# Seven products instead of eight in the second MLP matrix of a decoder trunk, with weight sums formed by adding DMAs

## Chip, cores and metric

One core of one Trainium2 chip runs the whole program. The metric is device time in microseconds (us); lower is better. Engines: PE = TensorE, DVE = VectorE, ACT = ScalarE, POOL = GpSimd, SP = SyncE, which only issues DMAs here.

## The reference

Two layers over 1,024 positions of width 1,024, in float32. Layer 0 mixes by sliding-window attention beside a gated delta rule, layer 1 by a gated recurrence (RG-LRU). Every layer ends with the same MLP of width 4,096, which the change is about:

```python
def sqrelu_mlp(x, w1, w2):
    h = jax.nn.relu(x @ w1)
    return (h * h) @ w2

def reference(x, ...):
    for layer in range(DEPTH):
        ...
        x = layer_norm(DN_ALPHA * x + mix, ln1_g[layer], ln1_b[layer])
        x = layer_norm(DN_ALPHA * x + sqrelu_mlp(x, mlp_w1[layer], mlp_w2[layer]), ln2_g[layer], ln2_b[layer])
    return x
```

## The kernel before

The sequence is cut into two halves of 512 positions (c = 0 and 1). Each half is a Python generator (`stream`): hybrid mixer, layer norm, MLP, recurrent mixer, layer norm, MLP, layer norm. A driver at the end of the function steps the generators and, between them, small ones (`mixers`: attention, delta rule, layer norms). It takes the half in the lower phase first whenever that one is not blocked, so one half's mixer lies among the other half's MLP products. A class `Clock` keeps rough times of all engines and fixes the order of PE's instructions; the other engines' instructions are put in order by the framework's scheduler.

Every matrix product of float32 values is done as three products of float32r values: each operand is split into a high part (a cast) and a low part (the operand minus its high part), and `mm3` multiplies high by high, high by low and low by high into one PSUM bank.

Weights come in blocks of 512 KB (128 partitions x 1,024 columns). `wblock` (line 339) loads a block on SP's queue into one of three buffers `ws`, then for each half of 512 columns casts it to `wh` (ACT, every fifth on DVE) and subtracts into `wl` (POOL and DVE in turn). Two blocks' split parts exist at a time.

The MLP (`mlp`, line 500) runs over eight groups e of 512 hidden columns. A group makes four tiles of hidden values from `w1` (24 products each, `proj_fm`), squares and splits them (ACT, POOL, DVE), and multiplies them by four blocks of `w2`, 24 products per block, into four PSUM banks for each half of the output; DVE adds a finished bank to the residual `y`. All products here have 512 columns. In the last group of the last half the output is finished row block by row block, so that the layer norm and the stores follow at once.

## Time and profile before

| | |
|---|---|
| three runs | 2,387.39, 2,388.78 and 2,389.77 us, median 2,388.78 |
| the profiled execution | span 2,384.5 us; its own time is not listed apart from the span |
| PE busy | 2,298.9 us, 96% |
| DVE, ACT, POOL busy | 1,345.1, 912.7 and 843.0 us |
| DMA | 227.43 MB, 95 GB/s on average |

The span runs from the first instruction to the last of one profiled execution. Busy time is the time in which an engine has at least one instruction running; matrix products overlap in a pipeline, so the length of one is more than the time from one to the next. Views named below: the page (busy times, queues), windows (busy time of each engine in a stretch, with the number of its instructions behind an x, the granted clock as a share of 2.4 GHz, the DMA engines' busy share and GB/s), groups by line (count, busy us and mean ns of one, then the idle time before them and what ended it), the waits, and the timeline.

### The profile page before, as it was taken

The numbers are of one execution on the slowest core, as the hardware profiler recorded it, in microseconds if no ns is written. First come the engines' busy times: TensorE is split into PE (matmuls) and PEld (weight loads), VectorE is DVE, ScalarE is ACT, GpSimd is POOL, SyncE is SP. The second block draws the span as 40 slices with busy tenths as digits, with TensorE's granted clock in tenths as the row PEclk, the third lists the DMA queues.
The fourth block names the chain that finished last, engine by engine and source line by source line (L and its number), as shares of the span: only waits on it lengthen the run. The fifth ranks groups of instructions, "written<-read, shape, count | busy, mean of one in ns | idle before, by whom it ended". The sixth has DMA issues, their size and how long they took to land. (4 is left out here: it accounts for less than half of the span.)

```text
span 2384.5 us, 33354 instructions
## 1 busy us (share of the span) xinstructions
PE 2298.9 (96%) x12724; PEld 1841.9 (77%) x12724; DVE 1345.1 (56%) x2550; ACT 912.7 (38%) x1813; POOL 843.0 (35%) x706
## 2 busy tenths in 40 slices
PE   8889997999999999999999999999999999999997
PEld 7666775677777878778887788877887788778876
DVE  7697659565754463755664623565665543633345
ACT  5364424443333242454443322344554232322331
POOL 3342334232332243433443432343333333433341
PEclk9999998999999999999999999999999999999999
DMA  4121231122233222322333222232325222332231
GB/s 154 54 81 31 81 124 36 54 69 74 73 114 110 95 88 98 123 89 97 98 131 125 82 96 97 97 121 91 98 93 177 85 97 97 107 115 98 98 117 51
DMA packets 67487, 227.43 MB, mean 95 GB/s; under 512 B 7424, under 2 KB 7808, under 8 KB 67328
## 3 DMA queue, kind: packets, MB, share of 16 engines
q1 hardware_dynamic: 58832, 204.01, 25.9%
q10 hardware_dynamic: 8496, 21.30, 2.5%
q8 instruction: 100, 1.64, 0.3%
q14 instruction: 59, 0.48, 0.1%
HBM read 216.89 MB, written 8.39 MB: 94 GB/s over the span
## 5 line engine op out<-in xcount | busy, mean ns | idle before, releaser
L177 POOL TENSOR_TENSOR wl<-ws,wh 128x512 fp32r<-128x512 f32 (+1 forms) x372 | 497.6, 1338 | 1261.4 <-ACT wh L177 979.4
L204 PE MATMUL mm<-g,wh 128*128 128x512 f32 x2816 | 886.7, 396 | 0.5 <-DVE g L177 0.5
L177 ACT CAST wh<-ws 128x512 fp32r<-128x512 f32 (+1 forms) x595 | 365.5, 616 | 993.0 <-PE mm L204 910.1
L204 PE MATMUL mm<-wh,s 128*128 128x512 f32 x1984 | 648.2, 399 | 11.4 <-ACT s L177 5.7
L204 PEld LDWEIGHTS mm<-g,wh 128*128 128x128 f32 x2816 | 520.2, 189 | 107.2 <-issue 2.9
L204 PE MATMUL mm<-g,wl 128*128 128x512 f32 x1408 | 550.9, 391 | 5.4 <-POOL wl L177 5.4
L204 PEld LDWEIGHTS mm<-wh,s 128*128 128x128 f32 x1984 | 374.0, 189 | 102.6 <-ACT s L177 6.2
L204 PE MATMUL mm<-wl,s 128*128 128x512 f32 x992 | 391.9, 395 | 2.3 <-POOL wl L177 1.4
L177 DVE TENSOR_TENSOR wl<-ws,wh 128x512 fp32r<-128x512 f32 (+1 forms) x372 | 281.2, 756 | 188.8 <-ACT wh L177 184.4
L204 PEld LDWEIGHTS mm<-g,wl 128*128 128x128 f32 x1408 | 265.1, 188 | 64.0 <-POOL wl L177 7.1
L204 PE MATMUL mm<-wh,g 128*128 128x512 f32 (+1 forms) x768 | 235.2, 380 | 10.0 <-ACT wh L177 6.1
L177 DVE TENSOR_TENSOR s<-s,s 128x512 fp32r<-128x512 f32 x128 | 100.4, 784 | 242.9 <-POOL s L177 231.1
L204 PEld LDWEIGHTS mm<-wl,s 128*128 128x128 f32 x992 | 187.4, 189 | 43.3 <-POOL wl L177 1.8
L177 DVE TENSOR_TENSOR g<-g,mm 128x512 f32<-128x512 f32 x224 | 144.0, 680 | 130.7 <-PE mm L204 130.5
L204 PEld LDWEIGHTS mm<-wh,g 128*128 128x128 f32 x768 | 142.0, 190 | 38.7 <-ACT wh L177 6.1
L177 DVE CAST wh<-ws 128x512 fp32r<-128x512 f32 (+1 forms) x149 | 73.8, 495 | 172.6 <-PE mm L204 165.0
L177 POOL TENSOR_TENSOR s<-s 128x512 f32<-128x512 f32 x128 | 145.3, 1135 | 26.4 <-ACT s L177 26.4
L204 PE MATMUL mm<-wl,g 128*128 128x512 f32 (+1 forms) x384 | 143.7, 374 | 0.1
L177 ACT ACTIVATE s<-mm 128x512 f32<-128x512 f32 x128 | 75.9, 593 | 62.1 <-PE mm L204 61.9
L177 ACT ACTIVATE s<-s 128x512 fp32r<-128x512 f32 (+1 forms) x136 | 83.5, 614 | 19.0 <-DVE s L177 8.0
L204 PEld LDWEIGHTS mm<-wl,g 128*128 128x128 f32 x384 | 72.9, 190 | 11.9 <-DVE wl L177 0.4
L204 PE MATMUL mx<-g,wh 128*128 128x512 f32 x256 | 78.8, 389 | 0.0
(209 smaller groups left out, 2230.3 us busy)
## 6 DMA issues: line engine op xcount, KB each, us to landing
ws<-w SPq DMA_DIRECT2D x256, 512.0 KB, 3.3
ws<-hin_fm SPq DMA_DIRECT2D x32, 512.0 KB, 3.3
ws<-rin SPq DMA_DIRECT2D x32, 512.0 KB, 3.3
ws<-hout SPq DMA_DIRECT2D x16, 512.0 KB, 3.4
ws<-rout SPq DMA_DIRECT2D x16, 512.0 KB, 3.4
t<-ln ACTq DMA_DIRECT2D x28, 256.0 KB, 4.2
ws<-hin_q SPq DMA_DIRECT2D x8, 512.0 KB, 3.2
g<-x ACTq DMA_DIRECT2D x8, 512.0 KB, 5.0
```

The costliest lines, as they stand in the source:

```text
L177: r = f(*a, **k)
L204: return self._pe(self.pe.matmul(out, lhsT, rhs, start=start, stop=stop), out, [lhsT, rhs], c, start)
```

## The change

A block of `w2` with 1,024 hidden rows (j = 0 to 3) is cut into four quarters b11, b12, b21, b22, and the hidden values of a half into a11 to a22 (first index: rows of positions, second: hidden columns). Eight products of such quarters become seven, after Winograd's form of Strassen's scheme (`seven`): four of the seven take sums of quarters of the weights: t1 = b11 + b12, t3 = b12 + b22, t2 = b11 + b12 + b22, t4 = all four. The signs are carried by the sums of activations and by `accumulate`.

- The sums t1 to t4 are formed in DRAM, once for each layer and j (`w2_sums`): SP copies a quarter (1 MB) into the sum's place, then POOL issues one to three DMAs that add another quarter to it, in rows of 8 KB; 32 copies and 56 adding DMAs in all. They are put one by one, by the model clock, from the first MLP of half 0 on.
- `hidden` makes eight tiles of hidden values per j and keeps them unsplit in two large buffers; `seven` forms the sums of activations on DVE, splits what it needs (cast on ACT, subtraction on DVE) and multiplies. One weight block now serves 12 products. Weight blocks of both are split with `pool=False`: the subtraction is on DVE.
- `weave` alternates one unit of the next group's first matrix with two units of this group's seven products. A unit is one weight block. The last j of a pass has no next group to be woven with, except in the last pass, where four hidden tiles of the last group (`ends`) stand in.
- Where not enough large buffers are free, or the other half is not yet past its output projection, a group goes the old way (`straight`). In the built program 11 of 16 groups (two layers, two halves, four j) take the seven products.
- `wblock` casts and subtracts 1,024 columns at once, and three blocks' split parts are kept.
- The recurrent blocks of half 0 and half 1 now run side by side (half 1 waits for the same block of half 0), after the first MLP of half 1; the layer norm ahead of half 1's MLP waits until half 0's first matrix is done, and the one ahead of half 0's recurrent mixer for the same of half 1.
- The scratch for DMA descriptors is set to 1,024 bytes per partition.

```diff
-WB, HV, LG = 4, 5, 2
-RINGS = dict(t=11, s=9, f=4)
+WB, WS, HV, LG = 3, 3, 5, 2
+RINGS = dict(t=11, s=10, f=4)
...
+    def split(h, l, x, key):
+        wcount[0] += 1
+        (V.tensor_copy if wcount[0] % HV == 0 else S.copy)(h, x)
+        (G if key else V).tensor_tensor(l, x, h, ALU.subtract)
+    def wblock(src, n=1024, hl=None, pool=True):
+        st = clk.tile("ws", WS, wpool.tile([P, 1024], F32, tag="ws", name=nm("ws"), bufs=WS))[:, :n]
+        DS.dma_start(st if len(src.shape) == 2 else st.rearrange("p (q c) -> p q c", q=2), src)
+        if hl is None:
+            hl = [clk.tile(t, WB, wpool.tile([P, 1024], F32R, tag=t, name=nm(t), bufs=WB))[:, :n] for t in ("wh", "wl")]
+        h, l = hl
+        split(h, l, st, pool and wcount[0] % LG)
...
+    SUMS = dict(t1=("b11", "b12"), t3=("b12", "b22"), t2=("b11", "b12", "b22"), t4=("b11", "b12", "b22", "b21"))
+    QUARTER = dict(b11=0, b12=1, b22=2, b21=3)
...
+    def w2_sums():
+        rows = lambda x: x.rearrange("(a b) c -> a (b c)", b=2)
+        behind = lambda i: tc.add_manual_dep(i.ins, PE.last.ins.name, NOSYNC, reason="not before")
+        for layer, j in ((i, j) for i in range(2) for j in range(4)):
+            for k, (first, *_) in SUMS.items():
+                behind(DS.dma_start(rows(tsum[layer][j][k]), rows(w2_quarter(layer, j, first))))
+                t = clk.now + 4.0
+                yield lambda: t
+            for i in range(1, 4):
+                for k, v in SUMS.items():
+                    if i < len(v):
+                        t = clk.now + 5.0
+                        yield lambda: t
+                        behind(DG.dma_start(rows(tsum[layer][j][k]), rows(w2_quarter(layer, j, v[i])), accum_op=ALU.add,
+                                            max_dma_last_dim=8192))
+            summed.add((layer, j))
...
+        def hidden(f, z):
+            ps = yield from proj_fm(w1[f], yT, mm_ps, False)
+            used()
+            S.activation(z, ps, AF.Relu)
+            S.activation(z, z, AF.Square)
...
+            yield from wait(lambda: (layer, j) in summed)
+            A = {f"a{r + 1}{q + 1}": v4(g[q])[:, :, r * 256:(r + 1) * 256] for q in range(2) for r in range(2)}
+            bank = {}
+            for i, (a, b, acc, out, sign, last) in enumerate((
+                    ("a12", "b21", "R", (0, 0), 1, False), ("a11", "b11", "X", (0, 0), 1, True),
+                    ("a21", "t1", "R", (1, 1), 1, False), ("a21", "t2", "X", (0, 1), -1, False),
+                    ("a12", "b22", "R", (0, 1), 1, True), ("a21", "t3", "X", (1, 1), -1, True),
+                    ("a22", "t4", "X", (1, 0), 1, True))):
+                if i == 2:
+                    V.tensor_tensor(A["a21"], A["a21"], A["a22"], ALU.subtract)
+                elif i == 3:
+                    V.tensor_tensor(A["a21"], A["a21"], A["a11"], ALU.subtract)
+                elif i == 4:
+                    V.tensor_tensor(A["a12"], A["a12"], A["a21"], ALU.add)
+                elif i == 5:
+                    V.scalar_tensor_tensor(A["a21"], A["a21"], -1.0, A["a22"], ALU.mult, ALU.subtract)
+                start = i < 3
+                if start:
+                    bank[acc] = [(mm_ps if acc == "X" else mx_ps)() for _ in range(2)]
+                    kept[0] += 2 * (acc == "X")
+                for p in range(2):
+                    yield from wait(lambda: either(2))
+                    ring = either(2)
+                    ah, al = ts(ring, F32R), ts(ring, F32R)
+                    ah2, al2 = (z.rearrange("p (k t) -> p k t", k=2) for z in (ah, al))
+                    x = A[a][:, 2 * p:2 * p + 2]
+                    S.copy(ah2, x)
+                    V.tensor_tensor(al2, x, ah2, ALU.subtract)
+                    wh, wl = wblock(w2_quarter(layer, j, b)[p * P:(p + 1) * P], pool=False)
+                    for k in range(2):
+                        for t in range(2):
+                            mm3(bank[acc][t], ah2[:, k, t * P:(t + 1) * P], al2[:, k, t * P:(t + 1) * P], wh[k], wl[k],
+                                start and p + k == 0, p + k == 2, not start)
+                            if p + k == 2:
+                                accumulate(bank[acc][t], 2 * out[0] + t, out[1], sign, done and last)
+                            if k + t < 2:
+                                yield
+                    free(ring, ah, al)
...
+        def weave(a, b, every):
+            left = [(a, 1), (b, every)] if a is not None else [(b, every)]
...
+        if res is not None:
+            yield from straight(6, False)
+        while e < 8 and not ((c == 1 or sts[1].get("op", -1) >= layer) and rings["g"] >= 2 and e % 2 == 0):
+            yield from straight(e, e == 7)
+            e += 1
+        if e < 8:
+            n = 3 if res is not None else 4
+            yield from first(e // 2)
+            for j in range(e // 2, n):
+                nxt = first(j + 1) if j + 1 < n else ends() if res is not None else None
+                yield from weave(nxt, seven(j, hids.pop(j), j == 3), 2)
+        if res is not None:
+            yield from finish()
...
+                if c == 0:
+                    yield from wait(lambda: "m7" in sts[1])
...
+        if c == 0:
+            spawn(w2_sums())
...
+            yield from wait(lambda: c == 0 or sts[0].get("rb", 0) > b)
...
+    nc = _bacc.Bacc("TRN2", target_bir_lowering=False, num_devices=1, dynamic_dma_scratch_size=1024)
```

How this moves instructions, at three places. Names are those of the built program; a number behind a name counts buffers, and the sums' names lose their first digit: t_0_0_105 is t1 of layer 0 and j = 0, 106 is t3, 107 t2, 108 t4.

SP's queue in the first MLP of half 0, before: weight loads (`ws`) alone, each waiting for a free buffer.

```order
L177 DMA ws_4748<-w_0 128x1024
L177 DMA ws_4799<-w_0 128x1024
L177 DMA ws_4875<-w_0 128x1024
L177 DMA ws_4971<-w_0 128x1024
L177 DMA ws_5037<-w_0 128x1024
```

And the same queue at that place now:

```order
L178 DMA t_0_0_105<-w_0 16x16384
L178 DMA t_0_0_106<-w_0 16x16384
L178 DMA t_0_0_107<-w_0 16x16384
L178 DMA ws_4721<-w_0 128x1024
L178 DMA t_0_0_108<-w_0 16x16384
L178 DMA ws_4830<-w_0 128x1024
L178 DMA ws_4872<-w_0 128x1024
L178 DMA ws_4923<-w_0 128x1024
```

Four copies of 1 MB from DRAM to DRAM stand among the loads; they wait for nothing, and four more follow for each further j.

POOL at the same place, before: subtractions for weights (`wl`), squares of hidden values (`s`) and attention work.

```order
L177 TENSOR_TENSOR wl_4646<-ws_4641,wh_4645 128x512
L177 TENSOR_TENSOR s_4496<-s_4496 128x512
L177 TENSOR_TENSOR wl_4753<-ws_4748,wh_4752 128x512
L177 TENSOR_TENSOR s_4601<-s_4601 128x512
L177 TENSOR_TENSOR g_115<-g_115,asc_4609 128x512
L177 TENSOR_TENSOR wl_4804<-ws_4799,wh_4803 128x512
```

And now (the squares' buffers are named `r`):

```order
L178 DMA t_0_0_105<-w_0 128x2048
L178 TENSOR_TENSOR wl_4651<-ws_4648,wh_4650 128x1024
L178 TENSOR_TENSOR r_4456<-r_4456 128x512
L178 DMA t_0_0_106<-w_0 128x2048
L178 DMA t_0_0_107<-w_0 128x2048
L178 TENSOR_TENSOR g_147<-g_147,asc_4474 128x512
L178 DMA t_0_0_108<-w_0 128x2048
L178 TENSOR_TENSOR r_4582<-r_4582 128x512
L178 TENSOR_TENSOR wl_4833<-ws_4830,wh_4832 128x1024
L178 DMA t_0_0_107<-w_0 128x2048
L178 TENSOR_TENSOR t_5040<-csb,dsc_3156 128x512
L178 DMA t_0_0_108<-w_0 128x2048 x2
```

The adding DMAs stand among the splits. The second addition into t2 (107) and the second and third into t4 (108) wait on POOL until the one before them on that sum has landed, and what stands behind them waits too.

DVE in a last group of a pass, j = 3 of layer 1 in half 0, where no first-matrix unit is woven in (`g_15423` and `g_15424` hold the hidden values, `s` is an activation's low part, `g_12869` the output, `lns` its statistics):

```order
L178 TENSOR_TENSOR g_15423<-g_15423 128x4x256
L178 TENSOR_TENSOR g_15424<-g_15424,g_15423 128x4x256
L178 TENSOR_TENSOR g_12869<-g_12869,mm_16171 128x512
L178 TENSOR_TENSOR s_16324<-g_15423,s_16323 128x512
L178 TENSOR_TENSOR g_12869<-g_12869,mm_16172 128x512
L178 BN_STATS lns_13481<-g_12869 128x6
L178 TENSOR_TENSOR s_16346<-g_15423,s_16345 128x512
L178 TENSOR_TENSOR wl_16330<-ws_16327,wh_16329 128x1024
L178 BN_STATS lns_13481<-g_12869 128x6
L178 CAST wh_16351<-ws_16349 128x1024
L178 SCALAR_TENSOR_TENSOR g_15423<-g_15423,g_15424 128x4x256
L178 TENSOR_TENSOR s_16371<-g_15424,s_16370 128x512
```

Sums of activations, activation splits, weight splits, additions to the output and its statistics all stand on this one engine there; before, the sums and the activation splits did not exist and half of the weight splits were POOL's.

## Rows read from the trace of the kernel before

**Rows 1.** The page's busy times: busy us, share of the span, number of instructions.

```profile
span 2384.5 us, 33354 instructions
...
PE 2298.9 (96%) x12724; PEld 1841.9 (77%) x12724; DVE 1345.1 (56%) x2550; ACT 912.7 (38%) x1813; POOL 843.0 (35%) x706
```

**Rows 2.** Windows: three stages; busy PE, PEld, DVE, ACT, POOL; clock, DMA share, GB/s.

```profile
0.00:600.00 600.00, 552.44 (x4455) 421.06 (x4455) 423.09 (x1037) 260.20 (x709) 210.62 (x196) 0.98 0.23 76
600.00:2300.00 1700.00, 1675.70 (x7966) 1364.07 (x7966) 875.07 (x1411) 633.42 (x1073) 608.53 (x491) 1.00 0.31 103
2300.00:2384.50 84.50, 70.77 (x305) 56.73 (x303) 46.90 (x103) 19.09 (x31) 23.80 (x20) 0.95 0.24 81
```

**Rows 3.** Windows: a stretch that holds MLP work alone.

```profile
2150.00:2300.00 150.00, 150.00 (x656) 122.97 (x655) 47.16 (x78) 44.73 (x74) 50.06 (x42) 1.00 0.29 95
```

**Rows 4.** Groups by line: PE's products with the second MLP matrix.

```profile
L204 PE MATMUL mm<-wh,s 128*128 128x512 f32 x1984 | 648.2, 399 | 11.4 <-ACT s L177 5.7 <-ACT f L177 4.2 <-DVE g L177 1.4
...
L204 PE MATMUL mm<-wl,s 128*128 128x512 f32 x992 | 391.9, 395 | 2.3 <-POOL wl L177 1.4 <-DVE wl L177 0.9
...
L204 PE MATMUL mm<-g,s 128*128 128x512 f32 x96 | 22.8, 396 | 0.7 <-DVE s L177 0.7
```

**Rows 5.** Waits of PE: us in total, times, longest us.

```profile
PE mx L207 <- DVE g L177: 9.4, 5, 6.7
...
PE mm L204 <- POOL wl L177: 6.8, 5, 1.8
...
PE mm L204 <- ACT wh L177: 6.1, 1, 6.1
```

**Rows 6.** Waits of SP's queue.

```profile
SPq L177 <- POOL wl L177: 1232.6, 345, 18.8
```

**Rows 7.** Groups by line, shapes apart: splits of weights, and statistics.

```profile
L177 DVE TENSOR_TENSOR wl<-ws,wh 128x512 fp32r<-128x512 f32 x364 | 277.3, 762 | 187.3 <-ACT wh L177 182.9
...
L177 DVE CAST wh<-ws 128x512 fp32r<-128x512 f32 x146 | 72.9, 499 | 170.9 <-PE mm L204 163.3 <-PE mx L204 6.7 <-DMA ws<-w 0.7
...
L177 DVE BATCH_NORM_STATS2 lns<-g 128x6 f32<-128x512 f32 x64 | 42.1, 679 | 0.1
...
L177 DVE TENSOR_TENSOR wl<-ws,wh 128x264 fp32r<-128x264 f32 x8 | 3.9, 488 | 1.5 <-ACT wh L177 1.5
...
L177 ACT CAST wh<-ws 128x512 fp32r<-128x512 f32 x582 | 360.5, 620 | 991.1 <-PE mm L204 908.4 <-PE mx L204 51.8 <-issue 20.7
...
L177 ACT CAST wh<-ws 128x264 fp32r<-128x264 f32 x13 | 5.0, 409 | 1.8 <-PE mm L204 1.6 <-DMA ws<-hin_kv 0.2
...
L177 POOL TENSOR_TENSOR wl<-ws,wh 128x512 fp32r<-128x512 f32 x364 | 490.1, 1346 | 1228.0 <-ACT wh L177 951.7 <-DVE wh L177 140.5 <-PE mm L204 56.7
```

**Rows 8.** Timeline of DVE in that stretch: start us, length us, instruction.

```profile
2149.45 1.27 DVE L177 TENSOR_TENSOR g<-g,mm 128x512 f32<-128x512 f32 x2
...
2158.27 0.69 DVE L177 TENSOR_TENSOR s<-s,s 128x512 fp32r<-128x512 f32 x1 [4.45 <-POOL s L177]
2158.88 0.69 DVE L177 TENSOR_TENSOR wl<-ws,wh 128x512 fp32r<-128x512 f32 x1
```

**Rows 9.** Windows: a dense elementwise stretch, and recurrent blocks inside an MLP.

```profile
350.00:400.00 50.00, 38.91 (x273) 29.45 (x272) 46.62 (x107) 26.14 (x68) 22.42 (x17) 0.90 0.17 53
350.00:450.00 100.00, 84.11 (x716) 61.02 (x716) 81.03 (x198) 45.79 (x118) 39.06 (x30) 0.91 0.14 43
1000.00:1200.00 200.00, 197.90 (x865) 161.90 (x864) 109.09 (x144) 99.00 (x159) 71.42 (x67) 1.00 0.29 95
```

**Rows 10.** DMA: the loads' queue (packets, MB, share) and issues (KB, us to landing).

```profile
q1 hardware_dynamic: 58832, 204.01, 25.9%
...
ws<-w SPq DMA_DIRECT2D x256, 512.0 KB, 3.3
...
g<-y ACTq DMA_DIRECT2D x8, 512.0 KB, 6.3
```

**Rows 11.** Windows: from the first MLP on, where the sums will lie.

```profile
355.00:900.00 545.00, 523.68 (x3597) 408.30 (x3596) 332.40 (x726) 205.35 (x483) 185.53 (x151) 0.98 0.24 79
```

More of the change, by code (lines that the diff above doesn't have):

```diff
@@ new lines, in mlp, with accumulate, used, straight @@
+    def mlp(layer, c, yT, yg, ls, res=None):
+        w1 = I[f"w1_{layer}"]
+        seen = set()
+        def accumulate(ps, n, half, sign, done):
+            y = ytile(yg, n)[:, half * 512:(half + 1) * 512]
+            op = ALU.add if sign > 0 else ALU.subtract
+            if (n, half) not in seen:
+                seen.add((n, half))
+                V.scalar_tensor_tensor(y, y, ALPHA, ps, ALU.mult, op)
+            else:
+                V.tensor_tensor(y, y, ps, op)
+            if done:
+                V.bn_stats(ls[:, n, 6 * half:6 * half + 6], y)
+        either = lambda n: next((r for r in "st" if rings[r] >= n), None)
+        left = [32]
+        def used():
+            left[0] -= 1
+            if left[0] == 0:
+                yT.free()
+                st[c]["m7"] = layer
+        def straight(e, done):
+            j, i = divmod(e, 2)
+            yield from wait(lambda: either(8))
+            ring = either(8)
+            own = [(ts(ring, F32R), ts(ring, F32R)) for _ in range(4)]
@@ L544, in mlp @@
             for half in range(2):
+                yield from wait(lambda: kept[0] == 0)
                 ps = [mm_ps() for _ in range(NT)]
                 for p in range(2):
-                    wh, wl = wblock(w2[(e * 2 + half) * 2 + p])
-                    for j in range(2):
-                        f = 2 * p + j
+                    wh, wl = wblock(w2_quarter(layer, j, f"b{i + 1}{half + 1}")[p * P:(p + 1) * P])
+                    for k in range(2):
+                        h, l = own[2 * p + k]
@@ new lines, in first @@
+        def first(j):
+            yield from need("g", 2)
+            g = [gran() for _ in range(2)]
+            for f in range(8):
+                yield from hidden(j * 8 + f, v4(g[f // 4])[:, f % 4, :])
+            hids[j] = g
+        def weave(a, b, every):
+            left = [(a, 1), (b, every)] if a is not None else [(b, every)]
+            while left:
+                stuck = True
+                for gen, k in list(left):
+                    for _ in range(k):
+                        r = next(gen, "end")
+                        if r is BLOCK:
+                            break
+                        stuck = False
+                        while r is not UNIT and r != "end":
+                            yield r
+                            r = next(gen, "end")
+                        if r == "end":
+                            left.remove((gen, k))
+                            break
+                        yield UNIT
+                if stuck:
+                    yield BLOCK
@@ L570, in out_proj @@
         for half in range(2):
+            yield from wait(lambda: kept[0] == 0)
             ps = yield from proj_tm([w[half * 4 + i] for i in range(4)], oT, 512)
@@ L1001, in rec_block @@
             if j == 1:
-                free("t", *xch, *xcl)
-                reg[1] = [ts("t") for _ in range(4)]
+                free(ring, *xch, *xcl)
+                reg[1] = [ts(ring) for _ in range(4)]
             r, a, iv, w = reg[j]
@@ L1115, in hybrid, with mix_out @@
         yield from wait(lambda: st.get("mids") == 4 and st.get("att") == 4)
-    def mix_out(w, oT, resid, which, r, s, t):
+    def mix_out(w, oT, resid, which, r, s, t, hold):
         yield from after(t)
@@ L1122, in mix_out @@
         yield from out_proj(w, oT, resid, s["yg"], ls)
+        s["ln0"]["op"] = which // 2
         s["yT"] = ActT()
         f = dict()
+        yield from wait(hold)
         yield from need("g", 4)
```

195 lines of the change are left out of this document (94 added, 101 removed).

## The prediction

> **What bounds the kernel now.** I read the busy times first, then the span by stages, then what TensorE waits for, then the queues that feed it. TensorE (PE) is busy 96% of the span and the next engine, VectorE (DVE), 56% [rows 1]. By stages, PE lacks 47.6 us of the first 600 us, 24.3 us of the next 1,700 and 13.7 us of the last 84.5 [rows 2]: in the middle, where both MLPs lie, nothing but the count of its matrix products decides. In a stretch with MLP work alone it is never idle and does 656 products in 150 us, so one product of 512 columns costs 150/656 = 0.2287 us [rows 3]; its granted clock there is 1.00, the 2.4 GHz level. The 396 ns that the groups give for one product is its length in an overlapping pipeline and is not its price [rows 4]. The list of waits confirms it: PE's longest entries are 5 to 10 us in total, over the whole run [rows 5]. SyncE, which issues the weight loads, waits instead, 1,233 us in total behind one kind of split alone, for weight buffers to come free [rows 6]: loads are early, DMA is not the bound.
>
> **What the change removes.** The second matrix of the MLP takes 1,984 + 992 + 96 = 3,072 products, 192 for each of 16 groups (two layers, two halves of the sequence, four groups j) [rows 4]. Seven products instead of eight save 24 of a group's 192. The order counts 8,840 products of 512 columns before and 8,576 now: 264 fewer, so 11 of the 16 groups take the new way; the others keep eight (three in half 0 of layer 0, one each in the halves of layer 1). On PE nothing is added: the sums are formed elsewhere. **264 x 0.2287 = 60.4 us** come off the engine that sets the end. That is the whole gain; the rest of this part asks what is given back.
>
> **VectorE beside the products.** A weight block of 512 KB now serves 12 products (2.74 us) in the seven-product code, against 24 (5.49 us) elsewhere. Here the low part of every weight block is formed on DVE alone, over 1,024 columns. A 512-column subtraction takes 0.762 us on average and a 264-column one 0.488 [rows 7], which carried on gives 1.33 us for 1,024; where GpSimd (POOL) is quiet two 512-column ones start 0.61 us apart [rows 8], so twice that, 1.22 us, bounds it below. I take 1.2, as POOL makes no splits there. One unit (a block of 12 products) then costs DVE 1.2 + 0.61 for splitting the activations + 0.64 for one addition to the output (two take 1.27 us [rows 8]) + 4 x 1.2/14 = 0.34 for the four sums of activations + 0.18 for one weight cast in five (0.499 us at 512 columns [rows 7]) = 2.97 us. A round of the weave (one unit of the first matrix, two of the second) is 48 products, 10.98 us on PE and 2 x 2.97 + 1.38 = 7.3 us on DVE: 67%, covered. ScalarE has 3 casts of about 1.06 us (0.620 and 0.409 us at 512 and 264 columns [rows 7]), less the fifth on DVE, and four 512-column operations of some 0.62 us there, 5.0 us: covered. What is not covered is the last group of a pass, which has no next group to be woven with: 14 units x (2.97 + 8 x 0.679/14 for the statistics [rows 7]) = 47.0 us of DVE beside 14 x 2.74 = 38.4 us of PE. There are three such stretches, so 0 to 3 x 8.6 = 26 us; the order puts first-matrix or recurrent products of the other half between many of those units, so I take half, **13 us**.
>
> **The recurrent blocks.** Before, the four blocks of one half lay inside the other half's MLP: from 1,000 to 1,200 us DVE is busy 54% and PE loses 2 us [rows 9]. MLP alone keeps DVE 31% busy [rows 3]. About 3.5 blocks of 120 products fit there, 96 us of PE; the other 104 us of MLP explain 33 us of DVE, so a block brings (109 - 33)/3.5 = 22 us of DVE to 27 us of PE, 80%. In the changed order the blocks of both halves and the output projection follow one another for some 650 products, 150 us, with almost no MLP between. The row with DVE at that level, 350 to 450 us (81%), has PE idle 15.9 us of 100 [rows 9]: 0 to 24 us. Those 100 us are attention and delta-rule chains of small operations, the recurrent blocks are long operations of two independent halves; I take **10 us**.
>
> **The sums of weights.** 32 copies and 56 adding transfers of 1 MB each lie in the first MLP, from 351 us on in the old trace. On SyncE's queue a copy stands between weight loads and delays the next one by its length. The queue's share gives 0.259 x 2,384.5/204 = 3.03 us for 1 MB on all 16 engines [rows 10]. A load that lands 3 to 6 us later than its 3.3 us [rows 10] still comes within three raw and three split buffers of 5.49 us each: nothing. POOL issues the adding transfers and waits, in order, for the earlier transfer on the same sum; behind it stand half of the weight splits (1.35 us each at 512 columns [rows 7]). POOL is busy 185 of 545 us there [rows 11], so it has room. The order puts the seven transfers of a group about 26 products, 6 us, apart; with a latency L up to 12 us only the third addition into t4 waits, L - 6, eight times. No row shows a transfer that adds. Between 4.8 us (a 512 KB load of 3.3 plus half a MB more) and 12.6 us (twice the slowest 512 KB row, 6.3 us [rows 10]) it costs PE 0 to 10 us; I take **5 us**.
> The engines' load is the tighter bound: now 24% of 545 us = 131 us [rows 11], copies add 32 x 3.03 = 97, additions 56 x 3.03 = 170 if each moves its data once: 398 us, 73%. The Trainium skill (Collectives: The Full Stack, The bandwidth ceiling) says that a reducing transfer costs twice because it reads two sources; by that the additions would be 339 us and the load 567 of 545 us, a full queue, and this term some 22 us instead of 5. No run here shows which.
>
> **Edits at nothing.** Weight splits are done once per 1,024 columns instead of twice per 512, and three pairs are kept instead of two: up to 13 us could come back where PE waited for a split (6.8 and 6.1 us [rows 5]), or a few us be lost where the first half is wanted early; 0. The tail keeps its form (96 products, the layer norm behind each row block): 0.
>
> **Sum.** -60.4 + 13 + 10 + 5 = -32 us. The profiled execution's span is 2,384.5 us; its own time isn't listed, and the median of the runs is 4.3 us above the span. 2,388.8 - 32 gives **2,356 us**. Ends: everything hidden and the 13 us regained, 2,388.8 - 60.4 - 13 = 2,315; all upper costs (26 + 24 + 10), 2,388.
>
> **Rivals.**
> (A) *All of it stays hidden.* For it: 11 groups lie where PE now idles 1.4% of the time, and DVE has a third of each round free. Against it: three stretches where DVE has more work than PE. 2,388.8 - 60.4 = 2,328, or down to 2,315. Chance 0.25.
> (B) *The elementwise engines eat the gain.* DVE becomes the bound in the last groups and the recurrent stage, upper ends of both terms: 2,378 to 2,388. For it: DVE at 93% of PE's time costs PE 11 us in 50 [rows 9]. Against it: PE lost only 2 us where recurrent blocks lay in the MLP. Chance 0.10.
> (C) *The additions hold POOL, and POOL holds PE: slower.* The place is POOL's queue in the first MLP, where weight splits stand behind waiting transfers. Split weights reach three blocks ahead, 16.5 us. The second addition into t2 waits L - 12, the third into t4 L - 6; PE loses what of each is over 16.5 us, 8 times. The gain of 32 us is gone at 4 us per group, L = 26. At L = 30 it is 8 x (1.5 + 7.5) = 72 us more than my sum, 2,428; at L = 40, 8 x (11.5 + 17.5) = 232, 2,588. For it: nothing in the trace shows what an addition in DRAM costs, and eight descriptors of 8 KB per engine could each wait for a read before they write. Against it: L = 26 is twice the 12.6 us that I took as the upper bound, and POOL idles 360 of the 545 us. The Trainium skill (SBUF — State Buffer, SBUF: two separate sides) adds that a transfer issued from GpSimd can't have its descriptors written while VectorE runs an fp32 copy from SBUF to SBUF; no row here shows such a transfer. That would lengthen L by one cast. Chance 0.14.
> That the change doesn't remove the products can't be: the order counts them. That the sums come too late can't be either, short of (C): the first is read some 200 us of products after its last addition.
>
> **How the numbers follow.** My forecast has 0.51, 2,335 to 2,375. About 0.2% of this time, 5 us, can be told from no change: faster by more than that takes the forecast, (A) and 0.03 of (B), less 0.01 for what I have not thought of, 0.78; same 0.05, half of (B); slower 0.17, (C), the last 0.02 of (B) and that 0.01. The range takes in (A)'s 2,315 and reaches into (C) to 2,410; its own part for the likeliest is given above.
>
> **What would show it.** 264 fewer products at the same 0.229 us; PE idle in the middle stage up from 24 us to some 50, with DVE as the releaser, in the three last groups and around the recurrent blocks; SyncE's loads landing in 5 to 8 us in the first MLP and 3.3 us after it; POOL's waits for its own transfers at a few us each. I am wrong if POOL's waits in the first MLP are over 16 us each (C), if PE's idle in the recurrent stage exceeds 24 us, or if loads of the woven groups land late after the additions have ended.

## The result, and the profile after

The changed kernel takes 2,394.51 us (median of 20 runs, 2,386.87 to 2,399.96) against 2,388.02 us before (20 runs, 2,385.53 to 2,392.44): a ratio of 1.0027, 95% interval 1.0019 to 1.0034. It is **slower by 0.27%**, where the prediction said 2,356 us and faster.

The page's busy times, of the changed kernel's profiled execution:

```profile
span 2396.2 us, 32070 instructions
...
PE 2251.6 (94%) x12460; PEld 1809.3 (76%) x12460; DVE 1562.4 (65%) x2537; ACT 1004.8 (42%) x1723; POOL 551.8 (23%) x399
```

PE has exactly the 264 products fewer (12,460 against 12,724 [rows 1]), so the change does what it says. But PE's busy time fell by 47.3 us and not by 60.4, and its idle time rose from 85.6 us to 144.6. The windows say where; the first three rows answer to [rows 2], the fourth to [rows 3], the fifth to [rows 11], the rest is read on from there (columns as in [rows 2]):

```profile
0.00:600.00 600.00, 549.13 (x4431) 419.70 (x4431) 414.48 (x985) 251.48 (x650) 213.93 (x174) 0.97 0.41 121
600.00:2300.00 1700.00, 1619.74 (x7669) 1322.11 (x7669) 1075.07 (x1424) 721.10 (x1030) 335.31 (x224) 0.98 0.52 159
2300.00:2396.20 96.20, 82.70 (x363) 67.47 (x361) 72.81 (x130) 32.19 (x44) 2.56 (x2) 0.95 0.32 110
2150.00:2300.00 150.00, 150.00 (x663) 124.20 (x663) 93.29 (x107) 63.96 (x84) 5.58 (x2) 1.00 0.46 151
355.00:900.00 545.00, 515.79 (x3525) 399.30 (x3524) 322.38 (x665) 189.66 (x412) 201.90 (x152) 0.98 0.78 214
1300.00:1700.00 400.00, 358.49 (x1560) 292.19 (x1559) 292.11 (x342) 217.59 (x309) 146.60 (x97) 0.95 0.32 106
1400.00:1450.00 50.00, 25.86 (x117) 21.43 (x116) 34.34 (x52) 25.47 (x38) 16.93 (x12) 0.73 0.32 114
750.00:1050.00 300.00, 279.21 (x1196) 226.07 (x1196) 173.88 (x233) 102.65 (x144) 71.71 (x56) 0.96 0.89 248
950.00:1000.00 50.00, 39.36 (x152) 30.42 (x151) 33.53 (x46) 14.48 (x18) 2.44 (x3) 0.90 0.87 272
```

In the middle stage PE now lacks 80.3 us instead of 24.3. The weave itself is not to blame: woven MLP does 663 products in 150 us with DVE 62% busy, even a little more than the 656 of before. Two places lose. From 1,300 to 1,700 us, where the recurrent blocks of both halves lie, PE idles 41.5 us; before, the same stretch of time lost 7.7 us. And where the sums are formed the DMA engines are at 0.78 of their time on average (0.24 before), 0.87 from 950 to 1,000 us, and PE loses 10.6 us in those 50. A lower granted clock goes with the gaps: a mean of 0.73 of full speed, so in part at the 1.2 GHz level and in part at the 2.4 GHz level, in the 50 us that hold the longest wait. The list of PE's waits has that one on top, and the list of all engines' waits has POOL's for its own transfers:

```profile
PE mx L210 <- DVE g L178: 34.3, 11, 24.1
```

```profile
POOL t L178 <- DMA t<-w: 165.7, 21, 27.3
```

The first are the transposes of a layer norm (L210), which stood 24.1 us behind DVE at 1,425 us, while nothing else was there for PE to do. The last has a wait as long as the rival (C) of the prediction asked for, 27.3 us, but it hardly reaches PE: PE waits for POOL's `wl` 2 us in the whole run. Of the DMA issues in the whole run and, below, from 750 to 1,020 us (KB, median us to landing):

```profile
ws<-w SPq DMA_DIRECT2D x234, 512.0 KB, 3.3
t<-w POOLq DMA_DIRECT2D x56, 1024.0 KB, 10.9
ws<-t SPq DMA_DIRECT2D x88, 512.0 KB, 3.3
...
t<-w POOLq DMA_DIRECT2D x25, 1024.0 KB, 11.8
ws<-w SPq DMA_DIRECT2D x33, 512.0 KB, 7.6
ws<-t SPq DMA_DIRECT2D x8, 512.0 KB, 8.3
```

An adding transfer of 1 MB lands after 10.9 us, inside the bounds 4.8 to 12.6 that the prediction took; loads of weights beside them land after 7.6 and 8.3 us instead of 3.3.

How a late load reaches PE can be followed at 980 us, in the last group of half 0's first MLP. It is the one group by seven products that lies beside the additions; the next begins as the last addition is issued, at 1,039 us (start us, length us, instruction, idle before it and what ended that):

```profile
982.50 1.04 ACT L178 CAST wh<-ws 128x1024 fp32r<-128x1024 f32 x1 [7.10 <-DMA ws<-t]
983.58 1.23 DVE L178 TENSOR_TENSOR wl<-ws,wh 128x1024 fp32r<-128x1024 f32 x1 [4.15 <-ACT wh L178]
985.46 1.28 DVE L178 TENSOR_TENSOR g<-g,mm 128x512 f32<-128x512 f32 x2
986.28 0.77 PE L206 MATMUL mm<-wh,s 128*128 128x512 f32 x1 [5.53 <-DVE g L178]
992.50 0.69 DVE L178 CAST wh<-ws 128x1024 fp32r<-128x1024 f32 x1 [5.17 <-DMA ws<-t]
```

A load (`ws<-t`) comes late, ACT waits 7.1 us for it before it can cast, DVE 4.2 us for the cast, the additions that empty PE's banks stand behind that split on DVE, and PE waits 5.5 us for them; the next load comes late too.

### The profile page after: what moved, and what is told of

It reads as the page before. It is cut to its first block, busy times and chain, and to the rows that moved or that the text cites. A ratio compares the mean times of both kernels' runs of the same rounds, so it can differ in the third digit from the quotient of the medians.

```text
span 2396.2 us, 32070 instructions
## 1 busy us (share of the span) xinstructions
PE 2251.6 (94%) x12460; PEld 1809.3 (76%) x12460; DVE 1562.4 (65%) x2537; ACT 1004.8 (42%) x1723; POOL 551.8 (23%) x399
## 3 DMA queue, kind: packets, MB, share of 16 engines
q0 software_dynamic: 8064, 58.72, 12.4%
## 4 chain that ended last, share of the span: by engine, by line
PE 67%; DVE 20%; ACT 4%; issue 3%; DMA 3%; POOL 1%; ACTq 0%; DVEq 0%; POOLq 0%
PE mm L206 52%; PE mx L206 13%; DVE g L178 7%; DVE t L178 3%; DVE s L178 2%; DVE wl L178 2%; DMA ws<-w 2%; DVE f L178 1%; DVE lnw L178 1%; PE mx L210 1%; DMA ws<-t 1%; DVE hsc L178 1%; ACT wh L178 1%; ACT t L178 1%; ACT g L178 1%
## 5 line engine op out<-in xcount | busy, mean ns | idle before, releaser
L178 ACT CAST wh<-ws 128x1024 fp32r<-128x1024 f32 (+1 forms) x350 | 364.8, 1042 | 735.8 <-PE mm L206 600.7
L178 DVE TENSOR_TENSOR wl<-ws,wh 128x1024 fp32r<-128x1024 f32 (+1 forms) x335 | 416.5, 1244 | 336.8 <-ACT wh L178 331.6
L178 POOL TENSOR_TENSOR wl<-ws,wh 128x1024 fp32r<-128x1024 f32 (+1 forms) x103 | 253.6, 2462 | 994.2 <-ACT wh L178 655.4
L206 PE MATMUL mm<-wh,s 128*128 128x512 f32 x1216 | 404.1, 400 | 19.3 <-DVE g L178 7.8
L206 PEld LDWEIGHTS mm<-wh,s 128*128 128x128 f32 x1216 | 232.0, 191 | 71.5 <-issue 5.9
L206 PE MATMUL mm<-wl,s 128*128 128x512 f32 x608 | 240.4, 395 | 1.8 <-DVE wl L178 1.7
L206 PE MATMUL mx<-wh,s 128*128 128x512 f32 x528 | 173.8, 396 | 3.1 <-DVE s L178 2.1
L178 DVE TENSOR_TENSOR s<-g,s 128x512 fp32r<-128x512 f32 x158 | 110.3, 714 | 42.5 <-ACT s L178 42.3
L206 PEld LDWEIGHTS mx<-wh,s 128*128 128x128 f32 x528 | 100.1, 190 | 25.3 <-DVE s L178 3.4
L206 PE MATMUL mx<-wl,s 128*128 128x512 f32 x264 | 103.7, 393 | 0.8 <-DVE wl L178 0.8
L210 PEld LDWEIGHTS mx<-csb,g 128*128 128x128 f32 x312 | 39.1, 152 | 70.3 <-DVE g L178 33.9
## 6 DMA issues: line engine op xcount, KB each, us to landing
t<-w POOLq DMA_DIRECT2D x56, 1024.0 KB, 10.9
```

The lines of the kernel that those rows point to most:

```text
L178: r = f(*a, **k)
L206: ins = self.pe.matmul(out, lhsT, rhs, start=start, stop=stop, skip_group_check=fresh)
L210: return self._pe(self.pe.transpose(out, x, ident), out, [x], 0.00042 * 2 * out.shape[-1])
```

## The experiments

Two theories stood at the start. **DMA**: the adding transfers fill the DMA engines, and weight loads come late. **Recurrence** (later called order): the changed waits take the MLP's products away from beside the recurrent blocks and layer norms. A third, **elementwise**: the seven products' splits overload DVE. Each result is a median with its ratio to the kernel before in the same batch and the ratio's 95% interval.

**e1**: the line `DG.dma_start(..., accum_op=ALU.add)` taken out.

> The changed kernel without its 56 adding transfers (the sums are left out, the 32 copies and every instruction of the five engines stay, the weight sums are therefore wrong). Theory DMA: the transfers crowd the queues and make the loads and GpSimd late; TensorE idles 17 us more than before between 700 and 1000 us, while the sums run, and that goes: about 2377 us (2370 to 2384). Theory recurrence: the loss lies between 1300 and 1700 us, where both halves' recurrent blocks run without a first MLP beside them (TensorE idles about 38 us more than before there); without the adding transfers the time stays at 2394 us (2389 to 2397).

2,367.12 us, 0.9912 (0.9899 to 0.9925). The additions cost **27.4 us**, more than the 17 that one stretch had shown; the time lies below the ranges of both theories. PE's instructions and their order are those of the change; followed by their count the two runs part by some 4 us up to 720 us, 15 by 960 and 29 by 1,020, and stay there. So about half of the loss, 14 us, comes within 60 us, in the group whose rows stand above (from 950 to 1,000 us PE idles 10.6 us in the change and 1.4 in e1); the other half comes mostly ahead of that group, where a block serves 24 products. The span differs by 29.1 us: 14.9 of idle time (129.7 against 144.6) and 14.2 of busy time (2,237.4 against 2,251.6 for the same products; the mean granted clock is 0.982 against 0.975). The recurrent stage keeps its loss, as the first of this kernel's waits of PE shows:

```profile
PE mx L210 <- DVE g L178: 32.6, 11, 24.1
```

**e2**: the same transfers 12 us apart, each group's set in the order of use.

```diff
-        for layer, j in ((i, j) for i in range(2) for j in range(4)):
+        for layer, j in ((0, 3), (0, 0), (0, 1), (0, 2), (1, 1), (1, 2), (1, 3), (1, 0)):
...
-                t = clk.now + 4.0
+                t = clk.now + 12.0
...
-                        t = clk.now + 5.0
+                        t = clk.now + 12.0
...
-            t = clk.now + 8.0
+            t = clk.now + 12.0
```

> The changed kernel with the same transfers set 12 us apart on the planner's clock in place of 4 to 8, and the sums of the four groups of a layer in the order in which they are read (last group first in layer 0, first group last in layer 1). Theory DMA: the busy share of the DMA engines falls from 0.9 to under 0.6 in 450 to 1050 us and most of the 17 us of idle time there goes: 2380 us (2374 to 2386). Theory recurrence: 2394 us (2389 to 2398), the gap of 24 us at 1401 to 1425 us stays.

2,378.08 us, 0.9963 (0.9952 to 0.9975). Sixteen of the 27 us come back by spacing and order alone, with the same bytes and the same additions. The gap before the layer norm stays.

**e3**: every group by `straight`, no `w2_sums`; the last group keeps its tail.

> The changed kernel's order, its waits, rings and 1024-wide splits, but all sixteen groups by plain products and no sums at all: 264 products more than the change, as many as before. Theory recurrence: what the order costs stays without the gain, so slower than before by the 38 us of added idle time of 1300 to 1700 us and a few us of lower clock: 2428 us (2412 to 2440). Theory DMA: the order costs nothing and the transfers are gone: 2388 us (2382 to 2396). Theory elementwise (the seven products' splits and additions on VectorE cause the idle time): 2388 us too, with VectorE's busy time back near 1345 us.

2,421.07 us, 1.0140 (1.0126 to 1.0155). With the products of before and no sums, the new order, rings and splits cost 33 us. DVE is busy for 1,293 us here, less than the 1,345 of before: the seven products' work on DVE can't make this loss.

**e4**: the kernel before, with `w2_sums` spawned at the same place and nobody reading the sums.

> The kernel before, its TensorE order unchanged, with the 32 copies and 56 adding transfers issued at the change's spacing and read by nobody. Theory DMA: the 17 us of 700 to 1000 us appear here: 2405 us (2396 to 2415). Theory recurrence: the transfers run beside the products and cost under 4 us: 2390 us (2386 to 2393).

2,392.13 us, 1.0015 (1.0006 to 1.0024): 4 us, below the DMA theory's range. The same additions that cost 27 us in the change cost little here, although they fill the DMA engines nearly as much, 0.86 of 750 to 1,050 us against 0.89, and loads of `w` from 750 to 1,020 us land after 6.1 us, against 7.6:

```profile
750.00:1050.00 300.00, 292.45 (x1311) 237.93 (x1310) 160.84 (x260) 100.09 (x171) 130.06 (x113) 1.00 0.86 238
```

So the DMA engines' share alone does not set the cost. What differs is how late a load may be: where a block serves 24 products, three buffers last 3 x 5.49 = 16.5 us, where it serves 12 they last 8.2 (estimates from [rows 3]), and about half of the change's loss lies in the one group of 12 beside the additions. That this is the reason is argued and not shown by an experiment: the additions were not put beside products of 24 per block in the change's order, rings and splits, and why the change also loses ahead of that group stays open.

**e6**: additions turned into plain copies of the same size in the same queue.

```diff
-                        behind(DG.dma_start(rows(tsum[layer][j][k]), rows(w2_quarter(layer, j, v[i])), accum_op=ALU.add,
-                                            max_dma_last_dim=8192))
+                        behind(DG.dma_start(rows(tsum[layer][j][k]), rows(w2_quarter(layer, j, v[i])), max_dma_last_dim=8192))
```

> The changed kernel with its 56 adding transfers turned into plain copies of the same size in the same queue at the same places (nothing is added, so the weight sums are wrong). Without them the kernel took 2367 us, with them 2394 us. Theory bandwidth: an adding MB holds the 16 DMA engines 5.1 us and a copied MB 2.9 us, so about half of the 27 us goes: 2380 us (2372 to 2387). Theory GpSimd queue: what costs is the waiting of GpSimd on the transfers' semaphores and the software queue itself: 2394 us (2388 to 2398).

2,374.27 us, 0.9942 (0.9928 to 0.9955). 20 of the 27 us were the adding as such, 7 the transfers' presence; five of these 7 are idle time from 950 to 1,000 us (6.4 us against 1.4 in e1), in the same group as above. The queues' rows, of the change and of e6 in turn (packets, MB, share of 16 engines' span), and the windows of 750 to 1,050 us of e1 and e6 (that of the change stands in the section on the result):

```profile
q0 software_dynamic: 8064, 58.72, 12.4%
```

```profile
q0 software_dynamic: 8064, 58.72, 6.7%
```

```profile
750.00:1050.00 300.00, 294.21 (x1304) 240.96 (x1304) 184.44 (x252) 112.41 (x155) 49.28 (x28) 0.99 0.45 164
```

```profile
750.00:1050.00 300.00, 288.96 (x1276) 235.85 (x1275) 182.44 (x251) 110.22 (x154) 64.07 (x55) 0.99 0.71 256
```

Same packets, same MB: 0.124 x 2,396.2 = 297 us of all 16 engines for adding, 0.067 x 2,372.3 = 159 for copying, a factor of 1.87. POOL's waits for its own transfers can't be the main cause: in e6 it waits for them 118.8 us, up to 39.4 at a time, and the time is within 7 us of e1.

**e7**: fewer additions, by building t2 from a copy of t1 and t4 from a copy of t2.

```diff
...
+            for o, x, add in (("t1", "b12", True), ("t3", "b22", True), ("t2", "t1", False),
+                              ("t2", "b22", True), ("t4", "t2", False), ("t4", "b21", True)):
+                t = clk.now + 12.0
...
+                if add:
+                    behind(DG.dma_start(q(o), q(x), accum_op=ALU.add, max_dma_last_dim=8192))
+                else:
+                    behind(DG.dma_start(q(o), q(x), max_dma_last_dim=8192))
```

> The changed kernel with the sums built on each other (t2 from a copy of t1, t4 from a copy of t2): 32 adding transfers in place of 56 and 32 copies as before, 12 us apart, sets in the order of use. Theory bandwidth: the spread-out sums took 2378 us with 56 adding transfers, 11 us over none at all; with 24 fewer 2371 us (2367 to 2377). Theory GpSimd queue: no better than 2378 us (2374 to 2386), since each transfer still waits for the one before.

2,370.19 us, 0.9932 (0.9919 to 0.9944): 3 us above no additions at all. Of the versions that compute the whole trunk this one and e13 (0.9922, 0.9910 to 0.9935) are the fastest, 0.7 to 0.8% under the kernel before; the two can't be told apart.

**e5**: e3 with the waits of the kernel before, and recurrent blocks of both halves one after the other.

```diff
-                    yield from wait(lambda: "m7" in sts[1])
...
+        if c == 0:
+            yield from wait(lambda: "ln0" in st[1])
+        else:
+            yield from wait(lambda: "rec" in st[0])
...
-            yield from wait(lambda: c == 0 or sts[0].get("rb", 0) > b)
```

> As the run with all groups straight (2421 us), but with the waits of the kernel before in place of the change's: the first half's layer norm and recurrent blocks start inside the second half's first MLP, and the second half's recurrent blocks after the first half's. 1024-wide splits, rings and products are those of that run. Theory order: the 33 us of that run are the price of the waits, so 2388 us (2384 to 2396). Theory elementwise: they are the price of the wide splits and of straight groups from either ring, so 2421 us (2415 to 2427).

2,401.32 us, 1.0055 (1.0043 to 1.0068). Between the two theories: the waits and the order of the recurrent blocks are 20 of the 33 us, and 13 are something else.

**e9**: e5 with the old splits, two of 512 columns and `WB = 4`.

> As the run with all groups straight and the waits of the kernel before (2401 us), but with the weight blocks split in halves of 512 columns and four buffers again. Theory wide splits: the 13 us above the kernel before (products wait 37.7 us for VectorE's additions that empty their banks, under 4 us before) come from VectorE and GpSimd standing longer behind one 1024-wide split, so 2388 us (2384 to 2393). Theory rings: they come from the straight groups' way of taking tiles and ending groups, so 2401 us (2396 to 2405).

2,410.90 us, 1.0098 (1.0083 to 1.0113). A miss for both theories: wide splits are worth 10 us here, and the cost beside them is larger. One place of the cost shows in e5's timeline (columns as in the timeline above):

```profile
1524.19 2.52 DVE L178 SCALAR_TENSOR_TENSOR g<-g,lnw,t 128x512 f32<-128x512 f32 x1 [1.60 <-DMA t<-ln]
1526.64 6.43 DVE L178 TENSOR_TENSOR g<-g,t 128x512 f32<-128x512 f32 x7
...
1529.62 0.33 ACTq L178 DMA_DIRECT2D t<-ln  x1
...
1532.99 1.80 DVE L178 SCALAR_TENSOR_TENSOR g<-g,lnw,t 128x512 f32<-128x512 f32 x1
1534.72 0.68 DVE L178 SCALAR_TENSOR_TENSOR g<-g,mm 128x512 f32<-128x512 f32 x1
...
1535.45 0.79 PE L206 MATMUL mm<-wh,t 128*128 128x512 f32 x1 [7.40 <-DVE g L178]
```

DVE waits 1.6 us for a layer norm's vector (`t<-ln`) and then does some 11 us of that layer norm in one piece; an addition that empties a product's bank stands behind it on DVE, and PE waits 7.4 us for that bank. Most of the wait is thus the layer norm's own work and not the late vector. The waiting product reads its hidden tile in `t`: the change lets straight groups use ring t, which held only layer norms and mixers before.

**e12**: e5 with straight groups in ring s alone.

```diff
-            yield from wait(lambda: either(8))
-            ring = either(8)
+            yield from need("s", 8)
+            ring = "s"
```

> As the run with all groups straight and the waits of the kernel before (2401 us; 2411 with narrow splits), but a straight group takes its eight hidden tiles from ring s alone, as in the kernel before, and leaves ring t to the layer norms and recurrent blocks. In the 2401 us run TensorE waits 7.4 us at 1535 us for an addition that stands on VectorE behind a layer norm whose vectors came late into ring t. Theory rings: the 13 us (23 with narrow splits) above the kernel before come from the layer norm's vectors waiting for tiles of ring t that a straight group holds: 2382 us (2376 to 2389), and the waits on VectorE's additions fall from 37.7 to about 15 us. Theory order: something else of the order costs them: 2401 us (2396 to 2405).

2,386.14 us, 0.9987 (0.9978 to 0.9996). 15 us gone, level with before. That the rings did it is shown; by which way, a vector late because its tile was still held or a layer norm that falls at another time, was not tried by itself.

**e15**: e3 with the straight groups of the second half in ring s, so that no product reads a hidden tile in ring t and the waits are alone.

> As the run with all groups straight and the change's waits (2421 us), but its straight groups of the second half take ring s alone; no product then reads a hidden tile in ring t. In the 2421 us run 192 products read ring t and wait 14.4 us for VectorE; in the change only 96 do, with 2.5 us. Theory rings: that wait belongs to the rings, so 2407 us (2402 to 2412), and the price of the change's waits by themselves is the difference to the 2386 us of the run with the waits of the kernel before and ring s alone: 21 us. Theory order: the waits move elsewhere, 2421 us (2416 to 2425).

2,415.47 us, 1.0114 (1.0097 to 1.0131): 6 us less than e3 where 14 were expected, outside both ranges, so most of the wait moved elsewhere. Against e12, which differs in the waits and the order of the recurrent blocks (the wait ahead of the second half's second MLP is in both), it is 29.3 us slower. From 1,300 to 1,700 us, of e12 and then e15:

```profile
1300.00:1700.00 400.00, 386.20 (x1710) 318.75 (x1709) 190.57 (x255) 134.69 (x182) 137.00 (x78) 0.98 0.27 95
```

```profile
1300.00:1700.00 400.00, 361.27 (x1569) 293.01 (x1568) 274.34 (x362) 223.03 (x316) 137.44 (x90) 0.95 0.32 110
```

With the waits DVE has 274 us of work in these 400 instead of 191, and PE 13.8 us of idle time becomes 38.7: both halves' recurrent blocks stand here, so that less MLP stands beside each of them.

**e16**: neither copies nor additions.

> The changed kernel with neither copies nor additions; the seven products read the first quarter of each sum from the weights (wrong sums, the same loads and the same instructions on the five engines). Theory DMA: the 32 copies cost some 3 us of the 16 engines each but lie in a queue that is under half full without additions, so 2366 us (2362 to 2368) beside 2367 us with them. Theory queue: on SyncE's queue each copy pushes the weight loads behind it back by its 8 us, so 2357 us (2350 to 2361).

2,366.43 us, 0.9906 (0.9891 to 0.9921), against 2,367.12 in e1: the 32 copies on SyncE's queue cost nothing that can be measured. From 750 to 1,050 us the DMA engines are busy for 0.35 here, 0.45 with the copies (e1) and 0.31 before: what the seven products load on top is little there, next to the additions.

**e8, e10, e11, e13, e14** trade products for order, with the sums of e7. The second half's first MLP takes n groups by seven products and the rest straight, and the first half's layer norm and recurrent blocks are let in beside the straight ones. e8 has n = 2; e10 lets the layer norm go when the last of these n begins; e11 is e10 with n = 1 (in these three a straight group may take ring t while no recurrent block runs), e13 is e10 with straight groups in ring s alone, e14 is e13 with n = 3. The edit of e10, in part:

```diff
-                    yield from wait(lambda: "m7" in sts[1])
+                    yield from wait(lambda: "half" in sts[1])
...
-            n = 3 if res is not None else 4
+            n = 3 if res is not None else 2 if (layer, c) == (0, 1) else 4
...
+                if (layer, c, j) == (0, 1, n - 1):
+                    st[c]["half"] = True
```

> A version that trades products for order: sums built on each other and spread out, seven products in eight groups (192 products fewer than before), the second half's first MLP with two seven-product groups and then two straight groups beside which the first half's layer norm and recurrent blocks run as in the kernel before. Theory order: the 33 us of the waits go, 192 products of 0.2287 us are saved and the sums cost some 5 us: 2353 us (2342 to 2366). Theory elementwise: the seven products' extra work on VectorE beside the recurrent blocks takes the saving away: 2375 us or more.

> The mixed version (2381 us) with the first half's layer norm let go one seven-product group earlier, when the last such group of the second half's first MLP begins; TensorE idled 23 us at 1400 to 1500 us in the mixed version, where both halves stood in their layer norms. Theory order: most of these 23 us go: 2362 us (2354 to 2372). Theory elementwise: VectorE is full beside that group and the recurrent blocks and the time stays: 2381 us (2375 to 2390).

> The same with only one seven-product group in the second half's first MLP and three straight groups behind it, so that the recurrent blocks have more products beside them (24 products more than the version before it, 5.5 us). Theory order: the gap is gone and only products count: 2366 us (2358 to 2376). Theory elementwise: less work on VectorE beside the recurrent blocks, so better than the version with two groups, by 5 us or more.

> The mixed version with the earlier layer norm (2376.5 us), its straight groups from ring s alone. Theory rings: the part of the loss that lies at 1500 to 1550 us and 950 to 1050 us (together 18 us of idle time) goes by half or more: 2364 us (2356 to 2371). Theory order: 2376 us (2371 to 2382).

> The mixed version with straight groups from ring s alone (2371.4 us, seven groups by seven products), now with three such groups in the second half's first MLP and one straight group behind them (nine in all, 48 products fewer, 11 us at 0.2287). Theory order: one straight group is too little to stand beside the first half's recurrent blocks, so a part of the 20 us of the change's waits comes back: 2370 us (2364 to 2380). Theory rings: once the rings are apart only products count: 2360 us (2356 to 2364).

e8: 2,381.37 us, 0.9977 (0.9967 to 0.9987). e10: 2,376.52, 0.9952 (0.9940 to 0.9964). e11: 2,380.60, 0.9962 (0.9950 to 0.9975). All three miss the order theory's forecast by 14 us or more. The elementwise theory's ranges hold e8 and e10; e11 goes against it, as it asked for 5 us less than e10 and got 4 more. So these three don't tell whether the seven products' work on DVE takes a part of the gain there. e13: 2,371.35, 0.9922 (0.9910 to 0.9935), 5 us better than e10 by the rings, where 12 were hoped for. e14: 2,383.97, 0.9983 (0.9974 to 0.9992), above the ranges of both theories: **48 products fewer than e13, which should give 11 us, and 12.6 us slower**. Of e13 and then e14, from 1,350 to 1,750 us:

```profile
1350.00:1750.00 400.00, 386.03 (x1704) 317.96 (x1703) 223.68 (x276) 160.36 (x222) 142.90 (x82) 0.98 0.27 94
```

```profile
1350.00:1750.00 400.00, 363.81 (x1590) 297.86 (x1589) 219.77 (x287) 168.51 (x233) 131.02 (x81) 0.95 0.28 99
```

PE loses 22 us more there with DVE no busier: the weights of one more j go by seven products, earlier, and the 384 products of its two straight groups no longer lie beside the chains of recurrent blocks and layer norms. What counts between these two is that there is other work for PE, not how full DVE is.

## Why the prediction was wrong

The runs make a ladder from the kernel before to the change, each step one part (medians; the intervals of the ratios leave some 3 us on each):

| part | runs | measured us | in the prediction |
|---|---|---|---|
| splits, rings and all else, straight groups in ring s | e12 against before (2,388.8) | -2.6 | 0 |
| the new waits, recurrent blocks side by side | e15 against e12 | +29.3 | +10 (0 to 24) |
| 264 products fewer, with what the seven products need | e16 against e15 | -49.0 | -60.4 + 13 = -47.4 |
| copies | e1 against e16 | +0.7 | 0 |
| additions | change against e1 | +27.4 | +5 (0 to 10) |

The parts add up to 5.8 us, the change's measured 6. That is no check of them, as each step starts where the one above it ended; and a part measured in another order of steps could come out differently.

- **The gain was right.** 60.4 us less 13 for groups without a partner was 47.4; 49.0 were measured, and a woven product costs 150/663 = 0.2262 us. The two terms show apart, too: from e15 to e16 PE's busy time falls by 63.7 us (2,296.4 to 2,232.7) and its idle time rises by 10.3 (117.3 to 127.6). In e1, undisturbed by additions, PE idles 3.0, 4.8 and 9.7 us about the three last groups (915 to 985, 1,245 to 1,345 and 1,960 to 2,045 us), with DVE busy for 85 to 90%; how much of the 11.4 given back the last groups cause was not tried by itself.
- **The adding DMAs: mis-sized, and the mechanism chosen wrongly.** The step that failed is that a load 3 to 6 us late "still comes within three raw and three split buffers of 5.49 us each: nothing", so that the price lay on POOL's queue alone. The additions' latency was in its bounds (10.9 us), the load was not: it counted an added MB once, 398 of 545 us, but the engines' time was 1.87 times a copy's. And 5.49 us is a block of 24 products; in the last group of half 0's first MLP, the one group by seven products beside the additions, a block lasts 2.74 us, and there PE stood behind single loads (ACT 7.1 us, PE 5.5) and lost about half of the 27.4. The other half was lost ahead of it, for a reason that stays open. The Trainium skill (Collectives: The Full Stack, The bandwidth ceiling) says of a collective's reducing step that it costs twice as it reads two sources; the trace comes close for this transfer, 1.87. The prediction gave 22 us by that rule and chose 5; 27.4 were measured, 28.1 with the copies. That the 22 came near is in part luck: it stood for a full queue, and e4 with nearly as full a queue lost 4.
- **The recurrent stage: right place, wrong size.** The step that failed is the choice of 10 us of 0 to 24 because the two halves' long operations would cover each other; 29.3 were measured, over its upper end. The row it went by (DVE 81% busy, PE idle 16% [rows 9]) gave that end. What it left out are the layer norms on both sides of the stage: they are serial chains, and the new waits put one where both halves stand, for 24.1 us in one piece. From 1,400 to 1,440 and from 1,600 to 1,620 us, about these two layer norms, lie 33.3 of the 41.5 us that PE idles; between 1,440 and 1,580 us, where the recurrent blocks lie, PE loses 5.7. Its own sign of error, more than 24 us of idle time there, came true.
- **Edits at nothing.** Wide splits gain, as the prediction allowed (up to 13 us): 9.6 us in e5 against e9. The second ring for straight groups was not in the sum at all; it costs 15 us in e5. In the change one straight group uses it, and its products waited 2.5 us, so it is a small part of this result.
- **The rivals.** (C) named the adding transfers as what makes it slower, with POOL's wait as the mechanism; POOL did wait up to 27 us, but with waits up to 39 us in e6 the time is within 7 us of e1. (B) named the recurrent stage as bound by the elementwise engines; e3 loses there without the seven products' work, and e14 against e13 says it is short of products beside chains, not short of DVE. Two small slips in these parts change nothing: at L = 26 the sum of (C) gives 3.5 us per group and not 4, and the 93% of (B) is DVE's share of the 50 us, not of PE's time.

Left open: why e8, e10 and e11 stayed 14 us or more over the order theory's forecasts (the rings explain 5 in e10), what the seven products give back on which engine, and why the additions cost the change so much more than the kernel before, beyond the group in which a block lasts half as long.

## What to carry to other kernels

A product that is taken away is worth its time only where other products stand behind it: count what lies beside every serial chain before letting the order change, since filler that was free becomes the bound. A cheaper algorithm that gets fewer products out of a loaded block shortens the time by which a load may be late. Price extra transfers against that time in the new kernel, and not by the DMA engines' share alone: at shares of 0.86 and 0.89 the same additions cost 4 us in the old kernel and 27 in the new. Spread such transfers over the time until they are needed, and replace additions by copies of partial sums: together this gave 24 of the 27 us back.

## What the runs showed of the hardware

An adding transfer from DRAM to DRAM holds the DMA engines 1.87 times as long as a copy of the same 58.72 MB in the same queue (297 against 159 us of 16 engines), and lands after 10.9 against 6.7 us for 1 MB. Spread out until 1,746 us, in e2, the adding transfers hold the engines as long (0.126 x 2,384.9 = 300 us), so crowding seems not to be what makes them long. Twenty runs of the change spread over 13.1 us (2,386.9 to 2,400.0), twenty of the kernel before over 6.9; that the additions do this is not shown. Half of what the additions cost PE is busy time and not idle time: 14.2 of 29.1 us, for the same products at a mean granted clock of 0.975 instead of 0.982.
